# Two blocks of a projection moved ahead of the norm that feeds them, with scale and shift applied to the banks

## The chip, the cores and the metric

The kernel runs on one core of one Trainium2 chip. The metric is device microseconds (us) of one execution; the time of a kernel is the median over runs. Below, PE is TensorE, DVE is VectorE, ACT is ScalarE, POOL is GpSimd, and SP is SyncE, whose queue issues nearly all transfers. PEld is TensorE's weight load, which the profile lists beside PE.

## The reference, cut to what matters

Two transformer blocks run one after the other on 512 tokens of width 1024. The end of the first block and the start of the second are what the change touches:

```python
# end of the first block
x = x + square(relu(hm @ w_up)) @ w_down
x = rms_norm(x, norm_final)
# start of the second block
ada = silu(c) @ w_ada + b_ada
shift, scale, gate = split(ada, 3)
h = _rms(x, g_pre) * (1.0 + scale) + shift
proj = h @ w_in
q, k, v, z_a, u_b, v_b, z_b, g_logits = split(proj, SPLIT_IDX, axis=-1)
q = _rope(q, positions); k = _rope(k, positions)
```

So h is, token by token, x times a factor for the column (norm_final, g_pre and 1 + scale), times a factor for the token (the two norms together), plus a shift for the column. The projection has 38 blocks of 128 columns; block 4 is k and block 5 is v.

## The kernel before

Activations are held feature-major: a tile is 128 features by 512 tokens, and X has eight such tiles. A product of 1024 features into one block of 128 columns is 24 matmuls into one bank, because each operand is split into a high and a low part (whi and wlo for weights, made by L167 on ACT and L168 on DVE) and three of the four products are kept (L193, L194, L195 in mm_fm). Weights come in halves of a block, 128x512 values: wload takes a raw buffer (five of them), issues its transfer on SP (L185) and splits it into whi (four buffers) and wlo (three).

The last quarter of the MLP (qt = 3) runs over eight column blocks j. For each, after the 24 matmuls, DVE scales the bank (L908), adds it to X (L912) and squares it with a weight (L914, tile wsq); ACT squares X (L715), and POOL adds up both kinds of squares (L716 for the norm of the MLP's result, L918 for the weighted sum, facc). Then come, in the text: sums over the features by one-column matmuls with a vector of ones (L161, first facc, then the last square, flast), an inverse square root of nine small DVE steps after two setting-up ones (L149 to L154), its broadcast over the partitions by matmuls into a bank (L203, rrb), and eight times three operations that make h2: hf (L931, DVE), its high part (L932, ACT), its low part (L933, DVE). Next 32 transposes of X (L939), whose banks ACT copies (L941) for eight transfers to memory (L942), and then the projection: block 4 (k, through rope), block 5 (v), blocks 0 to 3 (q) and the others.

A scheduler in the compiler orders each engine's instructions ahead of time: it takes the earliest in the text whose inputs it expects to be ready. The order on each engine is then fixed; an instruction that isn't ready holds up all behind it on that engine. Big tiles come from a pool of seven regions, banks for products from a pool of three (mm), for small sums from a pool of two (sc), for transposes from a pool of three (ch).

Of the kernel before, what the change touches and what calls it, by code (L numbers as in the profile page):

```python
# [10 lines left out]
F32 = mybir.dt.float32  # L11
# [35 lines left out]
def fused_kernel(ctx, tc, a, out):  # L47
# [19 lines left out]
    def regionr(name):  # L67
        return reg.tile([128, 4, 2, T], F32R, tag="R", bufs=7, name=nm(name))

    def tmp(tag, shape=(128, T), dt=F32, bufs=1):  # L70
        return tp.tile(list(shape), dt, tag=tag, bufs=bufs, name=nm(tag))

    def tt(name, shape=(128, T), dt=F32):
        return tp.tile(list(shape), dt, tag="t", bufs=10, name=nm(name))
# [4 lines left out]
    def mmbank():  # L79
        return ps.tile([128, T], F32, tag="mm", bufs=3, name=nm("mm"))  # L80

    def scbank():
        return ps.tile([128, T], F32, tag="sc", bufs=2, name=nm("sc"))
# [55 lines left out]
    def vcol(name, i=0, n=1):  # L139
        o = VOFF[name] + i  # L140
        return vc[:, o:o + n]
# [3 lines left out]
    def rsqrt(src, n, scale, eps, tag=None):  # L145
        v = tmp("rq_v", (128, n), bufs=2)
        y = tmp(tag or "rq_y", (128, n), bufs=1 if tag else 3)
        t = tmp("rq_t", (128, n), bufs=2)
        V.tensor_scalar(v, src, scale, eps, op0=ALU.mult, op1=ALU.add)  # L149
        V.tensor_scalar(y.bitcast(I32), v.bitcast(I32), -0.5, RSQRT_SEED, op0=ALU.mult, op1=ALU.add)  # L150
        for _ in range(3):
            V.tensor_tensor(t, y, y, op=ALU.mult)
            V.scalar_tensor_tensor(t, t, -0.5, v, op0=ALU.mult, op1=ALU.mult)
            V.scalar_tensor_tensor(y, t, 1.5, y, op0=ALU.add, op1=ALU.mult)  # L154
        return y

    def sums(*accs):
        p = scbank()
        for i, acc in enumerate(accs):
            for tb in range(TB):  # L160
                PE.matmul(p[:, tb:tb + 1], lhsT=acc[:, tb * 128:(tb + 1) * 128], rhs=ones,  # L161
                          start=i == 0 and tb == 0, stop=i == len(accs) - 1 and tb == TB - 1)
        return p[:, 0:TB]

    def split(src, hi, lo, scale=None, eng=V):
        if scale is None:
            S.copy(hi, src)  # L167
            eng.tensor_tensor(lo, src, hi.bitcast(F32), op=ALU.subtract)  # L168
        else:
            S.activation(hi, src, AF.Copy, scale=scale)  # L170
            V.scalar_tensor_tensor(lo, src, scale, hi.bitcast(F32), op0=ALU.mult, op1=ALU.subtract)

    def wsplit(raw, shape):
        hi = wp.tile(shape, F32R, tag="whi", bufs=4, name=nm("whi"))
        lo = wp.tile(shape, F32R, tag="wlo", bufs=3, name=nm("wlo"))
        split(raw, hi, lo)
        return hi, lo

    def wload(tiles, k0, nk):
        ncol = tiles.shape[2]  # L180
        step = T // ncol
        parts = []
        for k in range(k0, k0 + nk, step):
            raw = wp.tile([128, step, ncol], F32, tag="wraw", bufs=5, name=nm("wraw"))
            nc.sync.dma_start(raw, tiles[:, k:k + step, :])  # L185
            hi, lo = wsplit(raw, [128, step, ncol])
            parts += [(hi[:, i, :], lo[:, i, :]) for i in range(step)]
        return parts
# [8 lines left out]
    def pairs(regs, n):  # L197
        return [(regs[i // 4][:, i % 4, 0, :], regs[i // 4][:, i % 4, 1, :]) for i in range(n)]

    def bcast(r):  # L200
        p = scbank()
        for tb in range(TB):
            PE.matmul(p[:, tb * 128:(tb + 1) * 128], lhsT=r[:, tb:tb + 1].to_broadcast([128, 128]), rhs=ident,  # L203
                      start=True, stop=True)
        return p
# [662 lines left out]
    def rope_tables():  # L868
# [14 lines left out]
        V.tensor_scalar(ropeC, ropeC, -2.0, 1.0, op0=ALU.mult, op1=ALU.add)  # L883
        V.tensor_scalar(ropeS, ropeS, rsign, None, op0=ALU.mult)

    for qt in range(4):
        ffx = pairs([regionr("ff0"), regionr("ff1")], DB)
        for j in range(DB):
            p = mmbank()
            mm_fm(p, wload(a["w_up"][qt * DB + j], 0, DB), x2g)  # L890
            u = tt("u")
            S.activation(u, p, AF.Relu)
            sq_ins = V.tensor_tensor(u, u, u, op=ALU.mult)
            split(u, ffx[j][0], ffx[j][1])
            if qt == 0 and j == 0:
                r2 = rsqrt(sums(n2.acc), TB, 1.0 / D, 1e-6, "r2")
                V.tensor_tensor(r2, r2, r2, op=ALU.mult)
                S.copy(r2b, bcast(r2))
                rope_tables()
            if qt < 3:  # L900
                ada_step(qt * DB + j, sq_ins.ins)
            elif j == 0:
                late_constants()
        for j in range(DB):
            p = mmbank()
            mm_fm(p, wload(a["w_down"][j], qt * DB, DB), ffx)
            d = tt("d")
            V.tensor_tensor(d, p, r2b, op=ALU.mult)  # L908
            if qt < 3:
                G.tensor_tensor(X[:, j], X[:, j], d, op=ALU.add)  # L910
            else:
                V.tensor_tensor(X[:, j], X[:, j], d, op=ALU.add)  # L912
                sq = tt("wsq")
                V.scalar_tensor_tensor(sq, X[:, j], wf[:, j:j + 1], X[:, j], op0=ALU.mult, op1=ALU.mult)  # L914
                if j == 0:
                    facc = sq
                elif j < DB - 1:
                    G.tensor_tensor(facc, facc, sq, op=ALU.add)  # L918
                else:
                    flast = sq  # L920
                nf1.add(X[:, j])


    rrb = bcast(rsqrt(sums(facc, flast), TB, 1.0 / D, 1e-12))
    acol = cst.tile([128, DB], F32, name="acol")
    V.scalar_tensor_tensor(acol, adac[:, 8:16], 1.0, vcol("g_pre", 0, DB), op0=ALU.add, op1=ALU.mult)
    V.tensor_tensor(acol, acol, vcol("norm_final", 0, DB), op=ALU.mult)
    h2 = pairs([regionr("h2a"), regionr("h2b")], DB)
    for j in range(DB):
        hf = tt("hf")  # L930
# [14 lines left out]
    def proj2(blk):  # L945
        p = mmbank()
        mm_fm(p, wload(a["w_in_2"][blk], 0, DB), h2)
        return p

    def rope(p):  # L950
        f = tt("rf")
        S.copy(f, p)
        sw = tt("rsw")
        for p0 in (0, 32, 64, 96):
            nc.sync.dma_start(sw[p0:p0 + 32], f[p0 ^ 32:(p0 ^ 32) + 32])
        G.tensor_tensor(sw, sw, ropeS, op=ALU.mult)
        V.tensor_tensor(f, f, ropeC, op=ALU.mult)
        V.tensor_tensor(f, f, sw, op=ALU.add)
        return f
# [1 line left out]
    kvr = regionr("kvr")  # L961
    khi, klo = kvr[:, 0], kvr[:, 1]
    G.memset(klo.bitcast(F32), 0.0)
    f = rope(proj2(4))
    for kv in range(2):
        rows = slice(64 * kv, 64 * kv + 64)
        S.copy(khi[rows, kv], f[rows])
        S.copy(khi[64 - 64 * kv:128 - 64 * kv, kv], f[rows])
        V.tensor_tensor(klo[rows, kv], f[rows], khi[rows, kv].bitcast(F32), op=ALU.subtract)
    vf = tt("vf")  # L970
    S.copy(vf, proj2(5))
    pv = scbank()
    for tb in range(TB):
        PE.transpose(pv[:, tb * 128:(tb + 1) * 128], vf[:, tb * 128:(tb + 1) * 128], ident)
# [282 lines left out]
```

## Time and profile before

| | us |
|---|---|
| median of 3 runs | 1328.11 |
| lowest and highest | 1325.77, 1330.02 |
| profiled execution, its own time | 1321.5 |
| its span, first to last instruction | 1319.5 |
| PE busy | 1290.2 (98%) |
| DVE busy | 829.1 (63%) |
| ACT busy | 530.4 (40%) |
| POOL busy | 166.3 (13%) |
| mean granted clock of PE | 0.995 |

The span is shorter than the execution's own time by 2.0 us, which lie around it. PE's busy time counts the tail of each matmul, so a matmul shown with 0.39 us may be followed 0.23 us later by the next; how many of them start in a stretch tells more than the busy share. All positions below are us from the start of the span.

### The profile page before, as it was taken

Reading aid. Unit: us, or ns where it says so; the run is one execution under the profiler, and the core shown is the slowest. Engines: PE = TensorE matmul, PEld = TensorE weight load, DVE = VectorE, ACT = ScalarE, POOL = GpSimd, SP = SyncE. Lnnn points to the kernel's source line nnn. Section 1 sums busy time; section 2 is a strip of 40 time slices with the busy share of each in tenths; the row PEclk is TensorE's granted clock in tenths of the full one; section 3 lists DMA queues with packets and bytes.
Section 4 is the critical chain, followed back from the end, with each engine's and each line's share of the span. In section 5 each row is a group of like instructions: output and inputs, shape, how many; then the busy total and the mean of one; then the engine's idle time right before and its main releaser. Section 6 shows DMA issues by size and latency. Waiting matters only on the chain.

```text
span 1319.5 us, 18273 instructions
## 1 busy us (share of the span) xinstructions
PE 1290.2 (98%) x6594; PEld 1061.5 (80%) x6594; DVE 829.1 (63%) x1657; ACT 530.4 (40%) x956; POOL 166.3 (13%) x178
## 2 busy tenths in 40 slices
PE   8989999999999999999999999999999999999997
PEld 6778888878889888888888888888878777788886
DVE  6867585857477665656845636544677666663356
ACT  6534332322344443544523323324345465333342
POOL 1222101020110020002021020120232000100003
PEclk9989999999999999999999999999999999999999
DMA  6111432323324522143544535323334223233331
GB/s 233 56 56 59 115 102 67 98 59 115 95 66 137 195 98 83 56 161 122 190 128 129 191 97 165 110 92 96 96 120 143 74 70 130 88 96 97 97 118 64
DMA packets 85498, 143.95 MB, mean 109 GB/s; under 512 B 21504, under 2 KB 21632, under 8 KB 85408
## 3 DMA queue, kind: packets, MB, share of 16 engines
q1 hardware_dynamic: 85408, 142.78, 34.7%
q8 instruction: 52, 0.85, 0.3%
q14 instruction: 38, 0.31, 0.1%
HBM read 136.19 MB, written 5.24 MB: 107 GB/s over the span
## 4 chain that ended last, share of the span: by engine, by line
PE 93%; DVE 5%; issue 1%; POOL 0%; DMA 0%; ACT 0%; SPq 0%; DVEq 0%; ACTq 0%; POOLq 0%
PE mm L193 25%; PE mm L194 25%; PE mm L195 25%; PE mm L686 1%; PE mm L687 1%; PE mm L685 1%; PE sc L445 1%; DVE wlo L168 1%; PE ch L1046 1%; PE ch L517 1%; PE ch L1011 1%; PE ch L550 1%; PE ch L521 1%; PE ch L526 1%; PE ch L502 1%
## 5 line engine op out<-in xcount | busy, mean ns | idle before, releaser
L167 ACT CAST whi<-wraw 128x512 fp32r<-128x512 f32 x398 | 246.5, 622 | 518.7 <-PE mm L194 452.8
L168 DVE TENSOR_TENSOR wlo<-wraw,whi 128x512 fp32r<-128x512 f32 x398 | 291.4, 734 | 206.7 <-PE mm L195 105.4
L193 PE MATMUL mm<-h,whi 128*128 128x512 f32 x296 | 118.3, 400 | 0.0
L194 PE MATMUL mm<-h,whi 128*128 128x512 f32 x296 | 117.1, 396 | 0.0
L195 PE MATMUL mm<-h,wlo 128*128 128x512 f32 x296 | 116.6, 394 | 0.0
L193 PE MATMUL mm<-x2g,whi 128*128 128x512 f32 x256 | 100.2, 391 | 0.0
L195 PE MATMUL mm<-x2g,wlo 128*128 128x512 f32 x256 | 99.7, 390 | 0.0
L194 PE MATMUL mm<-x2g,whi 128*128 128x512 f32 x256 | 99.6, 389 | 0.0
L193 PE MATMUL mm<-ff,whi 128*128 128x512 f32 x256 | 99.6, 389 | 0.0
L194 PE MATMUL mm<-ff,whi 128*128 128x512 f32 x256 | 99.6, 389 | 0.0
L195 PE MATMUL mm<-ff,wlo 128*128 128x512 f32 x256 | 99.6, 389 | 0.0
L910 POOL TENSOR_TENSOR X<-X,d 128x512 f32<-128x512 f32 x24 | 39.3, 1636 | 220.9 <-DVE d L908 220.9
L193 PEld LDWEIGHTS mm<-h,whi 128*128 128x128 f32 x296 | 55.9, 189 | 13.6 <-DVE k L287 1.1
L195 PEld LDWEIGHTS mm<-h,wlo 128*128 128x128 f32 x296 | 55.9, 189 | 11.8 <-issue 0.2
L194 PEld LDWEIGHTS mm<-h,whi 128*128 128x128 f32 x296 | 55.9, 189 | 11.2 <-issue 0.2
L716 POOL TENSOR_TENSOR gt<-gt,nsq 128x512 f32<-128x512 f32 x21 | 27.7, 1321 | 274.9 <-ACT nsq L715 267.4
L194 PE MATMUL mm<-h2a,whi 128*128 128x512 f32 x152 | 59.8, 393 | 0.5 <-DVE h2a L933 0.5
L193 PE MATMUL mm<-h2a,whi 128*128 128x512 f32 x152 | 59.4, 393 | 0.3 <-ACT h2a L932 0.3
L195 PE MATMUL mm<-h2a,wlo 128*128 128x512 f32 x152 | 59.7, 393 | 0.0
L193 PE MATMUL mm<-h2b,whi 128*128 128x512 f32 x152 | 59.6, 392 | 0.0
L195 PE MATMUL mm<-h2b,wlo 128*128 128x512 f32 x152 | 59.5, 392 | 0.0
L194 PE MATMUL mm<-h2b,whi 128*128 128x512 f32 x152 | 59.3, 391 | 0.0
(488 smaller groups left out, 2777.7 us busy)
## 6 DMA issues: line engine op xcount, KB each, us to landing
wraw<-in_w_in SPq DMA_DIRECT2D x162, 256.0 KB, 2.7
wraw<-in_w_up SPq DMA_DIRECT2D x64, 256.0 KB, 2.6
wraw<-in_w_down SPq DMA_DIRECT2D x64, 256.0 KB, 2.7
adaraw<-in_w_ada SPq DMA_DIRECT2D x24, 512.0 KB, 3.6
wraw<-in_w_proj_b SPq DMA_DIRECT2D x16, 256.0 KB, 2.6
wraw<-in_w_k SPq DMA_DIRECT2D x16, 256.0 KB, 2.7
wraw<-in_w_proj_a SPq DMA_DIRECT2D x16, 256.0 KB, 2.8
wraw<-in_w_v SPq DMA_DIRECT2D x16, 256.0 KB, 2.7
```

The lines of the kernel that those rows point to most:

```text
L167: S.copy(hi, src)
L168: eng.tensor_tensor(lo, src, hi.bitcast(F32), op=ALU.subtract)
L193: PE.matmul(acc, lhsT=wh, rhs=xh, start=start and k == 0, stop=False)
L194: PE.matmul(acc, lhsT=wh, rhs=xl, start=False, stop=False)
L195: PE.matmul(acc, lhsT=wl, rhs=xh, start=False, stop=stop and k == n - 1)
L445: PE.matmul(pq[hd % 2][:, j * 128:(j + 1) * 128], lhsT=KB[p0:p0 + 64, j, n * 128:(n + 1) * 128], rhs=AR[p0:p0 + 64, j, n].rearrange("p q c ...
L502: PE.matmul(pg[ub:ub + 64, hd * 64:(hd + 1) * 64], lhsT=gr[:, hd, 0:64], rhs=VU[:, tb, c, hd, :], start=hd == 0, stop=n == 0 and hd == 7)
L517: PE.matmul(pu[ub:ub + 32, hs], lhsT=ZT[ub:ub + 32, c, hd, :], rhs=gsb[ub:ub + 32, hs], start=True, stop=True)
L521: PE.matmul(pg[ub + 32:ub + 64, hd * 64:(hd + 1) * 64], lhsT=gr[ub:ub + 32, hd, 32:64], rhs=VU[ub:ub + 32, tb, c, hd, :], start=False, sto ...
L526: PE.matmul(pu[ub + 32:ub + 64, hs], lhsT=ZT[ub + 32:ub + 64, c, hd, :], rhs=gsb[ub + 32:ub + 64, hs], start=True, stop=True)
L716: G.tensor_tensor(self.acc, self.acc, sq, op=ALU.add)
L910: G.tensor_tensor(X[:, j], X[:, j], d, op=ALU.add)
```

## The change

Two blocks of the second projection, 4 and 5, no longer wait for h2. During the last quarter of the MLP, each finished tile of X is multiplied by its column factor acol and split into a high and a low part (xa, two regions); acol is computed before that loop instead of after it. Blocks 4 and 5 are products of w_in_2 with xa. What that leaves out is applied afterwards: each bank is multiplied by the token's factor rrb on DVE, and the shift's product with the block's weights is added as a bias by ACT. That product is made on PE: 8 matmuls of a block's raw weights (128x128) with one column of the shift, into a bank from which DVE copies one column. rrb is now copied from its bank into SBUF by ACT. The text computes block 4 ahead of the broadcast, block 5 behind it, and h2 behind both. The other 36 blocks use h2 as before.

```diff
-    def wload(tiles, k0, nk):
+    def wload(tiles, k0, nk, use=None):
...
             nc.sync.dma_start(raw, tiles[:, k:k + step, :])
+            if use is not None:
+                use(raw, k)
             hi, lo = wsplit(raw, [128, step, ncol])
...
+    acol = cst.tile([128, DB], F32, name="acol")
+    xa = []
     for qt in range(4):
+        if qt == 3:
+            V.scalar_tensor_tensor(acol, adac[:, 8:16], 1.0, vcol("g_pre", 0, DB), op0=ALU.add, op1=ALU.mult)
+            V.tensor_tensor(acol, acol, vcol("norm_final", 0, DB), op=ALU.mult)
...
                 nf1.add(X[:, j])
-
-
-    rrb = bcast(rsqrt(sums(facc, flast), TB, 1.0 / D, 1e-12))
-    acol = cst.tile([128, DB], F32, name="acol")
-    V.scalar_tensor_tensor(acol, adac[:, 8:16], 1.0, vcol("g_pre", 0, DB), op0=ALU.add, op1=ALU.mult)
-    V.tensor_tensor(acol, acol, vcol("norm_final", 0, DB), op=ALU.mult)
+                if j == 0:
+                    xa = pairs([regionr("xa0"), regionr("xa1")], DB)
+                split(X[:, j], xa[j][0], xa[j][1], scale=acol[:, j:j + 1])
+
+
+    shifts = tmp("shifts", (128, 2))
+
+    def unscaled(i, blk):
+        pc = scbank()
+
+        def use(raw, k0):
+            for k in range(k0, k0 + 4):
+                PE.matmul(pc[:, 0:1], lhsT=raw[:, k - k0], rhs=adac[:, k:k + 1], start=k == 0, stop=k == DB - 1)
+
+        w = wload(a["w_in_2"][blk], 0, DB, use)
+        V.tensor_copy(shifts[:, i:i + 1], pc[:, 0:1])
+        p = mmbank()
+        mm_fm(p, w, xa)
+        return p
+
+    def rescaled(i, p):
+        f = tt("rf")
+        V.tensor_tensor(f, p, rrb, op=ALU.mult)
+        S.activation(f, f, AF.Identity, bias=shifts[:, i:i + 1])
+        return f
+
+    rr = rsqrt(sums(facc, flast), TB, 1.0 / D, 1e-12)
+    pk4 = unscaled(0, 4)
+    rrb = tt("rrb")
+    S.copy(rrb, bcast(rr))
+    pv5 = unscaled(1, 5)
     h2 = pairs([regionr("h2a"), regionr("h2b")], DB)
...
-    def rope(p):
-        f = tt("rf")
-        S.copy(f, p)
+    def rope(p, f=None):
+        if f is None:
+            f = tt("rf")
+            S.copy(f, p)
...
-    f = rope(proj2(4))
+    f = rope(None, rescaled(0, pk4))
...
-    vf = tt("vf")
-    S.copy(vf, proj2(5))
+    vf = rescaled(1, pv5)
```

## Rows read from the trace of the kernel before

**Rows 1.** The page: the chain that ended last, share of the span by engine.

```profile
PE 93%; DVE 5%; issue 1%; POOL 0%; DMA 0%; ACT 0%; SPq 0%; DVEq 0%; ACTq 0%; POOLq 0%
```

**Rows 2.** Timeline of PE: start, length, engine, line, operation, count, idle before.

```profile
966.96 0.39 PE L195 MATMUL mm<-ff,wlo 128*128 128x512 f32 x1
...
969.00 0.39 PE L195 MATMUL mm<-ff,wlo 128*128 128x512 f32 x1
969.91 1.05 PE L161 MATMUL sc<-ones,wsq 128*128 128x1 f32 x8 [0.52 <-POOL wsq L918]
970.82 1.51 PE L939 MATMUL ch<-ident,X 128*128 128x128 f32 x12
972.23 1.05 PE L161 MATMUL sc<-ones,wsq 128*128 128x1 f32 x8
973.15 1.71 PE L939 MATMUL ch<-ident,X 128*128 128x128 f32 x12
976.27 1.16 PE L203 MATMUL sc<-ident,rq_y 128*128 128x128 f32 x8 [1.41 <-DVE rq_y L154]
977.49 1.28 PE L939 MATMUL ch<-ident,X 128*128 128x128 f32 x8
979.10 0.73 PE L193 MATMUL mm<-h2a,whi 128*128 128x512 f32 x2 [0.34 <-ACT h2a L932]
...
985.02 0.39 PE L193 MATMUL mm<-h2b,whi 128*128 128x512 f32 x1
...
992.99 0.95 PE L161 MATMUL sc<-ones,gt 128*128 128x1 f32 x8
993.80 0.48 PE L194 MATMUL mm<-h2a,whi 128*128 128x512 f32 x1
```

**Rows 3.** L193, L194, L195 in a stretch: its length, PE busy (matmuls), clock, DMA share, GB/s.

```profile
969.20:985.00 15.80, 2.92 (x8) 1.00 0.43 156
...
969.20:985.00 15.80, 2.85 (x7) 1.00 0.43 156
...
969.20:985.00 15.80, 2.75 (x8) 1.00 0.43 156
```

**Rows 4.** Timeline of DVE: one block of the MLP's last quarter.

```profile
959.76 0.69 DVE L912 TENSOR_TENSOR X<-X,d 128x512 f32<-128x512 f32 x1
960.48 0.75 DVE L914 SCALAR_TENSOR_TENSOR wsq<-X,wf 128x512 f32<-128x512 f32 x1
961.33 1.84 DVE L168 TENSOR_TENSOR wlo<-wraw,whi 128x512 fp32r<-128x512 f32 x1
964.06 0.69 DVE L908 TENSOR_TENSOR d<-mm,gt 128x512 f32<-128x512 f32 x1 [0.89 <-PE mm L195]
964.67 0.68 DVE L168 TENSOR_TENSOR wlo<-wraw,whi 128x512 fp32r<-128x512 f32 x1
```

**Rows 5.** Timeline of POOL, same block.

```profile
961.32 1.30 POOL L716 TENSOR_TENSOR gt<-gt,nsq 128x512 f32<-128x512 f32 x1 [2.45 <-DVE wsq L914]
962.58 1.74 POOL L918 TENSOR_TENSOR wsq<-wsq,wsq 128x512 f32<-128x512 f32 x1
```

**Rows 6.** Timeline of DVE after that loop, to the end of h2.

```profile
971.43 0.75 DVE L914 SCALAR_TENSOR_TENSOR wsq<-X,wf 128x512 f32<-128x512 f32 x1
973.33 0.16 DVE L149 TENSOR_SCALAR rq_v<-sc 128x4 f32<-128x4 f32 x1 [1.15 <-PE sc L161]
...
977.54 2.07 DVE L931 SCALAR_TENSOR_TENSOR hf<-X,acol,sc 128x512 f32<-128x512 f32 x3 [1.33 <-PE sc L203]
...
987.39 1.50 DVE L933 SCALAR_TENSOR_TENSOR h2b<-hf,adac,h2b 128x512 fp32r<-128x512 f32 x2
```

**Rows 7.** Timeline of SP's queue.

```profile
972.62 9.57 SPq L942 DMA_DIRECT2D xf_d<-xo  x8
987.51 3.55 SPq L185 DMA_DIRECT2D wraw<-in_w_in  x3
```

**Rows 8.** L932 on ACT: count, duration in ns (least/median/most), first and last start.

```profile
L932 ACT ACTIVATE h2a<-hf,adac x4: 721/723/726, 978.3 to 982.3; 128x512 fp32r<-128x512 f32 x4
```

## The prediction

> **What bounds the kernel now.** I read the page's chain first: 93% of the span is PE, nearly nothing is transfers [rows 1]. So only what PE does, or waits for, counts, and I went to PE's timeline at the border between the MLP and the second projection [rows 2]. There the reader should look at starts, since a length holds the tail of a matmul. Inside the MLP ten matmuls start between 966.96 and 969.00, nine steps in 2.04 us: 0.227 us a matmul, 24 x 0.227 = 5.44 us a block, at a clock of 1.00 [rows 2, 3]. The last MLP matmul has its slot until 969.23. From 985.02 on PE is again in that step.
>
> In the 15.79 us between, 22 block matmuls start (23 are counted, one of them the tail of the 969.00 one) [rows 3]: 22 x 0.227 = 4.99 us. The sums are 16 entries, two for each of 8 matmuls, at (973.15 - 972.23) / 8 = 0.115 us: 1.84. The transposes are 12 + 12 + 8 at (972.23 - 970.82) / 12 = 0.118: 3.76. The broadcast is 8 entries, at the price of the sums 0.92 [rows 2]. Together 11.5, so PE stands idle for 15.8 - 11.5 = 4.3 us: at the end of the MLP for the POOL sum, while DVE does the inverse square root, and for the first pieces of h2. That is all the change can win here; 4.3 us is 0.33% of 1321.5.
>
> **What the change removes.** With xa of seven column blocks ready when the loop ends, PE has 21 matmuls of block 4 at hand (4.8 us) before it needs xa of the last one, then block 5. Its last tile of X is squared until 972.18 [rows 6]; ACT's part of the split (0.72, [rows 8]) and DVE's (0.75, as L914 [rows 4]) end near 974, and PE comes to it at 969.23 + 1.84 + 4.8 or later: covered. I keep the first wait, 969.23 to 969.91 for POOL [rows 2], because the sum of facc stands ahead of block 4 in the text: 0.7. Removed: 4.3 - 0.7 = 3.6 us; bounds 2.2 (see the order rival) and 4.3.
>
> **What it adds on PE.** Sixteen matmuls of 128x128 fp32 weights with one column. Their nearest row is the sum L161, the same shape: two entries each, 32 entries. The rows give 0.115 us an entry, or (993.80 - 992.99) / 8 = 0.101 where the next block's matmul follows [rows 2]. So 3.2 to 3.7 us; I take 3.6, since both rows within the gap give 0.114 and 0.115. PE is what sets the end here, so with the idle time gone nothing hides them. This is the heart of the forecast: one gap is filled, and three quarters of its length or more is paid again for the shift.
>
> The Trainium skill speaks of this price in "TensorE: Matmul & The Clock Gate", section Back-to-back issue gap: for 1 to 64 columns about 60 cycles, an issue floor of 25 ns. By that figure alone 32 entries would take 0.8 us, an estimate, and the sum would be 2.8 us lower; the rows of L161 do not bear it out. It is the third rival below.
>
> **What it adds in the MLP's loop.** Per block j one ACT operation of 0.72 us, which has room (ACT is busy for 40% of the span, and never the chain's engine [rows 1]), and one DVE operation of 0.75 us with two inputs in SBUF. DVE's idle time before L908 is 0.89 us a block, so at first sight it fits by 0.14 [rows 4]. But POOL stands in the way: L168 at 961.33 takes 1.84 us instead of 0.68, ending 0.55 us after POOL's L716 ends, and POOL's L918 in turn takes 1.74 [rows 4, 5]. Added up as if these excluded each other, a block has L912 0.69, L914 0.75 and two L168 of 0.68 on DVE, 2.80 us, and on POOL 1.30 and, from the end of L168 at 963.17 to 964.32, 1.15: 5.25 of 5.44 us. With 0.75 more it is 6.0, so 0.56 us too much in each of the six blocks that have both POOL operations, a lag of 3.4 us at the end. L168 is what PE could wait for: it ends at 963.17 and its first user is the fifth L195 of the next block, at 966.96 [rows 2, 4], 3.8 us later. So the lag stays inside the margin, if narrowly, and I put 0 for the loop; bounds 0 and 3.2 (rival below).
>
> The Trainium skill's page "GPSIMD Engine Reference", section Specifications, says that POOL's SBUF interfaces are shared with VectorE, with contention for DVE instructions that have two SBUF inputs; it would put all four of DVE's operations above, and the new one, against POOL. That speaks against this change, and the 1.84 us agree with it.
>
> **Behind the loop.** Half of the lag, 1.7 us, on DVE moves the last square to 973.9. From there as before: 1.15 to the first inverse-root step, 4.2 from that to the first hf [rows 6], 0.7 for ACT's new copy of rrb: 980.0. The sixteen DVE operations of h2 took 977.54 to 988.89 with one L168 among them, 10.7 without; with three splits of 0.68 h2 is whole at 992.7. PE meanwhile: 969.23 + 0.7 + 1.8 (sums) + 10.9 (blocks 4 and 5) + 3.6 + 0.9 = 987.1, and 990.9 after the transposes. Its first h2 block wants the last tile of h2 4.8 us later, at 995.7, or at 991.9 if the transposes are put behind: a wait of 0 or 0.8. I take 0.5. Then come two DVE passes of 0.69 over the banks; ACT's bias pass takes the place of a copy. The rope of block 4 is needed only by the attention, seven blocks on. The banks of 4 and 5 are let go near 994 instead of being copied at once; three mm banks let PE go on to the end of the first h2 block, 992 to 996, so this may cost a few tenths and no more.
>
> **Queues.** The raw tiles of the two blocks are held until PE has used them. Before, SP's next weight issue after the border came only at 987.51, behind the eight writes of X [rows 7], and PE didn't wait for weights. Now the first of the held buffers is free when PE has done half a block of one-column matmuls, near 971, sixteen us ahead of the first h2 block at 987: 0. If the transposes come late, the writes do too, and weights behind them on SP wait; three halves ahead are 3 x 2.72 = 8.2 us of cover.
>
> **Sum.** -3.6 + 3.6 + 0 + 0.5 = +0.5 us on the profiled 1321.5: 1322.0. The median of the runs lies 0.5% above the profiled execution (1328.11 to 1321.5), so the forecast on its scale is 1328.6.
>
> **The rivals.**
> *DVE and POOL saturate (slower).* If the new operation waits for a whole POOL operation of 1.3 each time, a block needs 0.75 + 1.3 - 0.89 = 1.16 us more than it has, 7.0 over six blocks, 3.2 beyond the 3.8 of margin: PE stalls on wlo, and h2 comes up to 2.9 us late behind it. +3.2 to +6.1, middle 4.7: 1326.2, or 1332.8 on the median's scale. It decides from 0.63 us of lag a block. For it: 5.25 of 5.44 already. Against: POOL's sums aren't urgent and can take the delay. Chance 0.22.
> *The order undoes it.* If PE's fixed order puts the second sum ahead of block 4, PE waits until 972.23 as now, with only the first sum to do: 2.1 us idle remain. Removed 2.2, added 3.6, and the 0.5: +1.9, 1323.4 or 1330.0. The scheduler already drew transposes ahead of that sum [rows 2], which speaks against it. Chance 0.12.
> *The one-column matmuls cost next to nothing (faster),* their weight loads going under the 512-column stream: -3.6 + 0 + 0.5 = -3.1, 1318.4 or 1325.0. For it: 0.101 instead of 0.115 where a block follows. Chance 0.08.
> *The balance above:* 0.58; its own range is -1.1 (all 4.3 removed, 3.2 paid) to +3.
>
> **Numbers.** A measurement here can't tell less than about 0.3%, 4 us, from no change. Faster takes a third of the third rival and little of the rest: 0.06. Slower takes most of the first rival, 0.17, and 0.05 of the others: 0.22. The same: 0.72. The range from 1324.5 to 1334.0 holds the balance and the order rival, most of the third and the first up to its upper part.
>
> **What the new profile should show.** L193 on xa starting within a microsecond or two of the last MLP matmul; no wait of PE for L154, L932 or L933; 32 new entries at 0.10 to 0.12 us; L168 or the new split at 1.3 us or more where POOL runs; wlo in time. I am wrong if PE waits for L168 inside the loop, if the first h2 block waits for L933, or if the new entries take 0.03 us.

## The result, and the profile after

The change made the kernel slower by half a per cent: 1333.99 us (median of 20 runs, 1327.65 to 1336.96) against 1327.38 for the kernel before (20 runs, 1321.11 to 1330.42). The ratio is 1.0051, interval 1.0036 to 1.0065, so 6.6 us. The time lies within the range that was given, at its upper end; the forecast itself, no measurable change, was wrong.

The profiled execution of after took 1329.73 us with a span of 1328.0, 8.5 more than before's. Line numbers of after: 195 to 197 are the three products of a block's matmul (193 to 195 before), 915, 919 and 921 DVE's three operations of a column block (908, 912, 914), 718 and 925 POOL's sums (716, 918), 171 the low part of xa, 941 the one-column matmuls with the shift, 944 the copy of their column, 205 the broadcast.

The chain that ended last, shares of the span, answers to [rows 1]:

```profile
PE 90%; DVE 7%; issue 1%; ACT 1%; POOL 0%; DMA 0%; SPq 0%; DVEq 0%; ACTq 0%; POOLq 0%
```

PE still sets the end, but DVE's share went up from 5 to 7%. The first block's whole MLP takes the same time in both (352.6 and 352.7 us from its first to its last matmul), and so does everything from the first score matmul of the second block's attention on (283.6 in both). Two stretches make up the 8.5 us. One is in the state scan of the first block, 4.1 us, where both kernels have the same instructions in the same order and only the granted clock differs:

```profile
200.00:300.00 100.00, 98.26 (x690) 80.85 (x689) 60.48 (x151) 26.63 (x45) 15.24 (x22) 0.96 0.27 71
```

The columns are the window, its length, busy time and count of PE, PE's weight loads, DVE, ACT and POOL, then PE's granted clock, the DMA share and GB/s. The clock is 0.96; in before's window it is 1.00, though the change touches nothing there. Both kernels' executions spread over some 10 us, and I count this with that spread and not with the change. The other 4.4 us lie between the last MLP matmul and the first score matmul: 66.9 us before (969.0 to 1035.9), 71.3 after (973.1 to 1044.4). The first score matmul, before and after:

```profile
1035.86 0.33 PE L1011 MATMUL ch<-kvr,qr 128*128 128x128 f32 x2
1044.43 0.33 PE L1043 MATMUL ch<-kvr,qr 128*128 128x128 f32 x2
```

Everything below is about this stretch.

PE's timeline there answers to [rows 2]; a bracket holds the recorded idle time and its releaser:

```profile
973.06 0.39 PE L197 MATMUL mm<-ff,wlo 128*128 128x512 f32 x1
974.71 1.05 PE L161 MATMUL sc<-ones,wsq 128*128 128x1 f32 x8 [1.26 <-POOL wsq L925]
975.63 1.93 PE L941 MATMUL sc<-adac,wraw 128*128 128x1 f32 x16
977.41 0.69 PE L195 MATMUL mm<-xa,whi 128*128 128x512 f32 x1
977.90 0.63 PE L196 MATMUL mm<-xa,whi 128*128 128x512 f32 x1
978.32 0.63 PE L197 MATMUL mm<-xa,wlo 128*128 128x512 f32 x1
...
981.14 0.40 PE L195 MATMUL mm<-xa,whi 128*128 128x512 f32 x1
...
986.72 1.16 PE L205 MATMUL sc<-ident,rq_y 128*128 128x128 f32 x8
987.72 1.84 PE L941 MATMUL sc<-adac,wraw 128*128 128x1 f32 x16
989.42 0.48 PE L197 MATMUL mm<-xa,wlo 128*128 128x512 f32 x1
...
1018.95 0.39 PE L196 MATMUL mm<-h2b,whi 128*128 128x512 f32 x1
1020.27 0.50 PE L197 MATMUL mm<-h2b,wlo 128*128 128x512 f32 x1 [0.93 <-DVE wlo L168]
```

Four things are to be seen, each measured from start to start with 0.227 us for a block matmul's slot, as in the prediction.

- **The wait for POOL** behind the MLP is there, twice as long: the last slot ends at 973.29, the sum starts at 974.71, so 1.42 us instead of 0.68.
- **The one-column matmuls** take 977.41 - 975.63 = 1.78 and 989.42 - 987.72 = 1.70 us for 16 entries each: 3.48.
- **The block matmuls behind them step at half pace**: from 977.41 to 981.14 nine of them take 3.73 us instead of 9 x 0.227 = 2.04, a loss of 1.69. The steps of 0.42 and 0.43 us are near twice 0.227.
- **A new wait for wlo** at 1020.27: 1020.27 - 1018.95 - 0.227 = 1.09 us.

That the pace is the clock is seen in the windows, with the columns as above:

```profile
968.00:974.00 6.00, 5.45 (x25) 4.17 (x23) 5.94 (x8) 2.86 (x5) 3.97 (x3) 1.00 0.06 24
974.00:980.00 6.00, 5.29 (x30) 4.74 (x31) 2.37 (x5) 0.94 (x2) 0.83 (x2) 0.79 0.24 76
980.00:986.00 6.00, 6.00 (x30) 5.05 (x29) 3.03 (x12) 1.45 (x3) 2.00 (x2) 0.92 0.04 14
986.00:992.00 6.00, 6.00 (x39) 5.12 (x38) 3.03 (x8) 2.22 (x5) 0.00 (x0) 1.00 0.40 128
```

The granted clock is full until the MLP's end, means of 0.79 and 0.92 stand in the next two windows, which is part of the time at the lower of its two levels (1.2 instead of 2.4 GHz), and then it is full again. In before it is 1.00 from 969.2 to 985 [rows 3], and in every later window of the stretch.

The sum: idle slots of before in this stretch come to 0.68 (POOL) + 1.72 (inverse root) + 0.28 (behind the broadcast) + 0.67 and 0.78 (first pieces of h2) = 4.13. After has 1.42 + 3.48 + 1.69 + 1.09 = 7.68, and 0.57 in three small gaps (0.13 ahead of the broadcast, 0.20 and 0.24 around transposes). 7.68 + 0.57 - 4.13 = +4.1 of the 4.4.

Why POOL is late is in the loop's timeline of DVE, which answers to [rows 4], and of POOL, to [rows 5]:

```profile
964.35 0.68 DVE L919 TENSOR_TENSOR X<-X,d 128x512 f32<-128x512 f32 x1
965.07 0.75 DVE L921 SCALAR_TENSOR_TENSOR wsq<-X,wf 128x512 f32<-128x512 f32 x1
965.74 0.68 DVE L168 TENSOR_TENSOR wlo<-wraw,whi 128x512 fp32r<-128x512 f32 x1
966.41 1.72 DVE L171 SCALAR_TENSOR_TENSOR xa<-X,acol,xa 128x512 fp32r<-128x512 f32 x1
968.12 0.69 DVE L915 TENSOR_TENSOR d<-mm,gt 128x512 f32<-128x512 f32 x1
968.73 1.11 DVE L168 TENSOR_TENSOR wlo<-wraw,whi 128x512 fp32r<-128x512 f32 x1
969.76 0.68 DVE L919 TENSOR_TENSOR X<-X,d 128x512 f32<-128x512 f32 x1
```

```profile
965.90 1.68 POOL L718 TENSOR_TENSOR gt<-gt,nsq 128x512 f32<-128x512 f32 x1 [2.02 <-DVE wsq L921]
967.54 1.74 POOL L925 TENSOR_TENSOR wsq<-wsq,wsq 128x512 f32<-128x512 f32 x1
971.31 1.67 POOL L718 TENSOR_TENSOR gt<-gt,nsq 128x512 f32<-128x512 f32 x1 [2.03 <-DVE wsq L921]
972.93 1.73 POOL L925 TENSOR_TENSOR wsq<-wsq,wsq 128x512 f32<-128x512 f32 x1
```

The split of xa meets POOL as L168 did before: 1.72 us instead of the 0.75 of L921, a form with as many operands. It ends 0.55 us after L718, as L168 ended 0.55 after L716 in [rows 4, 5]. DVE has no idle time left before L915. Yet it keeps pace: from one L919 to the next it is 969.76 - 964.35 = 5.41 us, no more than PE's 5.44 for a block. The L168 that stands beside POOL's first addition takes 0.68 now instead of 1.84; the split behind it is what is lengthened. POOL pays too. Two additions stand one behind the other after each square; the pair of this block takes 3.38 us, that of [rows 5] 3.00. The last pair is what PE's sum waits for. Before's was:

```profile
966.82 1.79 POOL L716 TENSOR_TENSOR gt<-gt,nsq 128x512 f32<-128x512 f32 x1 [2.51 <-DVE wsq L914]
968.57 1.29 POOL L918 TENSOR_TENSOR wsq<-wsq,wsq 128x512 f32<-128x512 f32 x1
```

It started 2.41 us ahead of the end of the MLP's last slot and took 3.04. After's started 1.98 ahead of it and took 3.35, to 974.66; PE's sum starts at 974.71. So 0.43 us of the longer wait are DVE's later square, and 0.31 are POOL's longer pair. The Trainium skill's "GPSIMD Engine Reference", section Specifications, tells of this contention without a size; here it is about 1 us for one DVE operation and 0.4 for a pair of POOL's additions.

### The profile page after: what moved, and what is told of

It is laid out like the page before. It is cut to its first block, busy times and chain, and to the rows that moved or that the text cites. A ratio compares the mean times of both kernels' runs of the same rounds, so it can differ in the third digit from the quotient of the medians.

```text
span 1328.0 us, 18354 instructions
## 1 busy us (share of the span) xinstructions
PE 1299.0 (98%) x6626; PEld 1068.7 (80%) x6626; DVE 837.6 (63%) x1669; ACT 535.4 (40%) x965; POOL 168.6 (13%) x178
## 4 chain that ended last, share of the span: by engine, by line
PE 90%; DVE 7%; issue 1%; ACT 1%; POOL 0%; DMA 0%; SPq 0%; DVEq 0%; ACTq 0%; POOLq 0%
PE mm L195 24%; PE mm L197 24%; PE mm L196 24%; DVE wlo L168 2%; PE mm L688 1%; PE mm L687 1%; PE mm L689 1%; PE sc L447 1%; PE ch L1078 1%; PE ch L519 1%; PE ch L528 1%; DVE xa L171 1%; PE ch L552 1%; PE ch L1043 1%; PE ch L523 1%
## 5 line engine op out<-in xcount | busy, mean ns | idle before, releaser
L168 DVE TENSOR_TENSOR wlo<-wraw,whi 128x512 fp32r<-128x512 f32 x398 | 289.4, 730 | 206.9 <-PE mm L197 106.1
L195 PE MATMUL mm<-h,whi 128*128 128x512 f32 x296 | 118.7, 401 | 0.0
L195 PE MATMUL mm<-x2g,whi 128*128 128x512 f32 x256 | 100.2, 391 | 0.0
L195 PE MATMUL mm<-ff,whi 128*128 128x512 f32 x256 | 99.6, 389 | 0.0
L195 PEld LDWEIGHTS mm<-h,whi 128*128 128x128 f32 x296 | 56.2, 190 | 13.7 <-DVE k L289 1.1
L718 POOL TENSOR_TENSOR gt<-gt,nsq 128x512 f32<-128x512 f32 x21 | 29.2, 1393 | 276.4 <-ACT nsq L717 270.3
L197 PE MATMUL mm<-h2b,wlo 128*128 128x512 f32 x144 | 56.7, 394 | 1.0 <-DVE wlo L168 0.9
L197 PE MATMUL mm<-h2a,wlo 128*128 128x512 f32 x144 | 56.6, 393 | 0.0
L195 PE MATMUL mm<-h2a,whi 128*128 128x512 f32 x144 | 56.6, 393 | 0.0
L195 PE MATMUL mm<-h2b,whi 128*128 128x512 f32 x144 | 56.6, 393 | 0.0
L196 PE MATMUL mm<-h2a,whi 128*128 128x512 f32 x144 | 56.5, 393 | 0.0
L196 PE MATMUL mm<-h2b,whi 128*128 128x512 f32 x144 | 56.4, 392 | 0.0
```

The lines of the kernel that those rows point to most:

```text
L195: PE.matmul(acc, lhsT=wh, rhs=xh, start=start and k == 0, stop=False)
L196: PE.matmul(acc, lhsT=wh, rhs=xl, start=False, stop=False)
L197: PE.matmul(acc, lhsT=wl, rhs=xh, start=False, stop=stop and k == n - 1)
L718: G.tensor_tensor(self.acc, self.acc, sq, op=ALU.add)
```

## The experiments

The ratios below are to the kernel before on the same chips, with 95% intervals. "Stretch" is from the last MLP matmul to the first score matmul in the profile, 66.9 us before and 71.3 after, with both starts read to 0.1 us. The last column has the granted clock of the two windows of 6 us that begin with the last MLP matmul (the first profile of after was shown above in windows that begin 1 us later, 0.79 and 0.92). One caution for the ratios: a kernel whose stretch is before's to 0.1 us (the fourteenth row) measured 1.0016, so two ratios that differ by 0.002 aren't told apart, and the stretch is the finer measure.

| kernel | median, us | before there | ratio | stretch | clock behind the MLP |
|---|---|---|---|---|---|
| after, first profile | 1333.99 | 1327.38 | 1.0051 [1.0036, 1.0065] | 71.3 | .87, .85 |
| after again, twice | 1326.49, 1329.45 (one run each) | 1327.6 | | 71.4, 73.0 | .85, .87; .71, .73 |
| after without the shift | 1327.55 | 1327.8 | 1.0011 [0.9993, 1.0030] | 67.4 | .81, .90 |
| before + split | 1330.11 | 1327.8 | 1.0016 [0.9998, 1.0035] | 68.8 | .82, .61 |
| before + one-column matmuls | 1330.18 | 1327.8 | 1.0018 [1.0000, 1.0035] | 69.4 | 1.00 |
| after, copies late | 1334.37 | 1327.8 | 1.0038 [1.0019, 1.0057] | 72.3 | .85, .87 |
| after, POOL's sum first | 1329.17 | 1326.24 | 1.0017 [0.9995, 1.0038] | 70.1 | .83, .89 |
| no shift, POOL's sum first | 1325.44 | 1326.24 | 0.9987 [0.9968, 1.0006] | 64.4 | 1.00 |
| one block on xa, POOL's sum first | 1325.26 | 1326.24 | 0.9996 [0.9976, 1.0016] | 66.2 | 1.00 |
| before, constants in the gap | 1329.19 | 1326.24 | 1.0017 [0.9998, 1.0037] | 70.4 | 1.00 |
| interleaved, POOL's sum first | 1337.11 | 1327.58 | 1.0073 [1.0046, 1.0100] | other order | 1.00 |
| interleaved | 1341.59 | 1327.58 | 1.0109 [1.0080, 1.0138] | other order | .84, .88 |
| before + split, POOL's sum first | 1322.88 | 1327.58 | 0.9983 [0.9963, 1.0003] | 66.9 | 1.00 |
| before, POOL's sum first | 1328.31 | 1327.58 | 1.0016 [0.9999, 1.0033] | 66.8 | 1.00 |
| interleaved, scores pinned | 1338.45 | 1327.6 | 1.0071 [1.0043, 1.0099] | 75.0 | 1.00 |
| columns behind each block, POOL's sum first | 1328.17 | 1327.18 | 1.0003 [0.9983, 1.0024] | 67.2 | 1.00 |

### First: which part costs

**After without the shift.** The one-column matmuls and their copies go; ACT adds another column, which costs the same. k and v lack the shift.

```diff
...
-                PE.matmul(pc[:, 0:1], lhsT=raw[:, k - k0], rhs=adac[:, k:k + 1], start=k == 0, stop=k == DB - 1)
-
-        w = wload(a["w_in_2"][blk], 0, DB, use)
-        V.tensor_copy(shifts[:, i:i + 1], pc[:, 0:1])
+        w = wload(a["w_in_2"][blk], 0, DB)
...
-        S.activation(f, f, AF.Identity, bias=shifts[:, i:i + 1])
+        S.activation(f, f, AF.Identity, bias=adac[:, i:i + 1])
```

> The change without the shift's product: the 16 one-column matmuls and the two copies of their column are left out, and the bias of blocks 4 and 5 is another column of the same size, so that k and v lack their shift. Theory 1 (the one-column matmuls are what costs: 32 entries of 0.11 us, 3.5 us, and behind them nine block matmuls at half the granted clock, 1.6 us): the changed kernel's excess of 6.6 us falls by 5 or more, to between -1 and +1.5 us against the kernel before, and the clock of the stretch behind the MLP stays 1.00. Theory 2 (the split's second operation in the MLP's loop is what costs, by DVE and POOL shutting each other out): the excess stays at +3 us or more. Theory 3 (the copies of the shift's column hold DVE's queue) expects a fall too, with DVE's two waits of 3.3 and 2.9 us gone; the next run but two tells it from theory 1.

The stretch is 67.4, 3.9 less than after's, near the 3.5 of the entries. Yet with 4.1 of idle time to win and nothing paid for the shift it should have been well under before's 66.9. PE waits 1.42 for POOL here too, and the clock fell:

```profile
975.30:981.30 6.00, 4.74 (x21) 3.69 (x20) 3.46 (x5) 1.87 (x3) 3.74 (x3) 0.81 0.28 85
```

**Before + split.** Only xa is made, and acol ahead of it; nobody uses xa.

```diff
...
                 nf1.add(X[:, j])
+                if j == 0:
+                    xa = pairs([regionr("xa0"), regionr("xa1")], DB)
+                split(X[:, j], xa[j][0], xa[j][1], scale=acol[:, j:j + 1])
```

> The kernel before, with only the scaled split of X into xa added to the MLP's last quarter (16 operations, nothing reads xa). Theory 1: within 1 us of the kernel before, since wlo has 3.8 us of margin. Theory 2: slower by 3 us or more. Either way the last MLP matmul is followed by a longer wait for POOL's sum than the 0.7 us of before, if the late sum (1.4 us in the changed kernel) comes from the split.

1.9 us of stretch. The wait for POOL is after's, with the sums and transposes behind it instead of one-column matmuls, and the clock falls there as well:

```profile
978.11 1.05 PE L161 MATMUL sc<-ones,wsq 128*128 128x1 f32 x8 [1.24 <-POOL wsq L923]
```

```profile
976.50:982.50 6.00, 4.76 (x33) 4.39 (x32) 3.78 (x8) 3.31 (x6) 3.73 (x3) 0.82 0.37 124
```

**Before + one-column matmuls**, ahead of blocks 4 and 5, which stay on h2.

```diff
+        if blk in (4, 5):
...
+            w = wload(a["w_in_2"][blk], 0, DB, use)
+            V.tensor_copy(shifts[:, blk - 4:blk - 3], pc[:, 0:1])
```

> The kernel before, with only the 16 one-column matmuls of blocks 4 and 5 and the two copies added (nothing reads the result). Theory 1: slower by about 3.5 us, less what falls into the 4.1 us in which PE stands idle there (the first eight may: then 1.8 to 3.5). If the half clock comes from such matmuls too, it shows in the window behind the MLP. Theory 2: within 1 us.

2.5 us of stretch, at full clock, for 32 entries: each sixteen take 1.71 us (984.43 to 986.14, 995.63 to 997.34), about what the rows of L161 said. Together that is 3.42, less what of before's idle time they cover, and nothing like the 0.8 of the third rival.

**After, copies late.** DVE's queue showed a suspect: the copy of the first block's column waits 3.34 us for PE, and the next one 2.93, with h2 behind it.

```profile
977.59 0.16 DVE L944 COPY shifts<-sc 128x1 f32<-128x1 f32 x1 [3.34 <-PE sc L941]
989.60 0.16 DVE L944 COPY shifts<-sc 128x1 f32<-128x1 f32 x1 [2.93 <-PE sc L941]
```

So both columns went to one bank, copied by one operation behind the last piece of h2.

```diff
...
-        V.tensor_copy(shifts[:, i:i + 1], pc[:, 0:1])
...
+        if i == 0:
+            with tc.issue_after(h2_ins.ins):
+                V.tensor_copy(shifts, pc[:, 0:2])
```

> The changed kernel, with the shift's two columns in one bank and copied in one operation put behind h2 on DVE, so that no copy stands ahead of the last tile of X or of h2 in DVE's queue. Theory 3 (the copies' wait costs): faster than the changed kernel by 2 us or more, h2 begins 6 us earlier. Theory 1: within 1 us of the changed kernel, because PE has blocks 4 and 5 to do meanwhile; the 32 entries and the half clock stay.

72.3 and 1.0038: no gain. The copies' waits of six us are gone, but h2 starts no earlier: 16.8 us behind the MLP's last slot, against 16.4 in after, because it waits for rrb now. This theory fell.

### Second: the wait, the clock and the columns

**After, POOL's sum first.** The addition of facc goes ahead of the other one on POOL; every other engine keeps its order.

```diff
-                    G.tensor_tensor(facc, facc, sq, op=ALU.add)
+                    fadd = G.tensor_tensor(facc, facc, sq, op=ALU.add)
...
-                nf1.add(X[:, j])
+                if j:
+                    with tc.issue_after(fadd.ins):
+                        nf1.add(X[:, j])
+                else:
+                    nf1.add(X[:, j])
```

> The changed kernel with one thing else: on POOL each addition to facc is put ahead of the addition for the MLP norm instead of behind it. Theory A (the split makes facc late on POOL, PE stands still for 1.4 us at the end of the MLP instead of 0.7, and the granted clock is halved behind that): PE's wait falls under 0.7 us, the clock of the 12 us behind the MLP is 1.00, and the stretch from the last MLP matmul to the first score matmul falls from 71.3 to 69 us or less; against the kernel before the excess falls from 6.6 to 3 to 4 us, the price of the columns. Theory B (the clock is halved because of the one-column matmuls): the wait falls, the clock stays halved for some 3 us and the stretch falls by 0.7 to 1 us only.

The wait is gone and the stretch is 1.2 us shorter, 70.1, but the clock fell all the same:

```profile
975.54 0.40 PE L197 MATMUL mm<-ff,wlo 128*128 128x512 f32 x1
975.78 0.95 PE L161 MATMUL sc<-ones,wsq 128*128 128x1 f32 x8
976.59 1.93 PE L945 MATMUL sc<-adac,wraw 128*128 128x1 f32 x16
```

```profile
975.50:981.50 6.00, 6.00 (x36) 5.28 (x36) 3.02 (x6) 1.86 (x3) 2.05 (x2) 0.83 0.32 90
981.50:987.50 6.00, 6.00 (x29) 4.92 (x27) 3.51 (x13) 1.24 (x2) 1.46 (x2) 0.89 0.00 0
```

Eight block matmuls from 979.39 to 982.73 took 3.34 us instead of 1.82, a loss of 1.5. By the profile PE is busy all through these windows. What stands in for the wait is 24 one-column entries in a row, 2.6 us from 975.78. So my theory that the wait alone brings the lower clock fell.

**The same without the shift** (k and v lack it) takes the columns away too.

> The change without the shift's product (16 one-column matmuls, two copies and the true bias left out) and with facc first on POOL. Theory A: clock 1.00 behind the MLP, stretch of 67.4 falling to 65 us or less, faster than the kernel before by 1 to 3 us. Theory B expects the clock back at 1.00 as well, but no more than that the run without columns had it, that is halved; then the stretch stays at 66.5 or more.

The clock stays at 1.00 and the stretch is 64.4: 2.5 under before's, in spite of a later wait of 1.13 us for split weights. This is the gain that the moved blocks have without the shift's price.

**One block on xa** (block 5 back on h2), the columns strewn between block 4's matmuls, the copy late, POOL's sum first.

```diff
...
-        mm_fm(p, w, xa)
+        for k in range(DB):
+            mm_fm(p, w[k:k + 1], xa[k:k + 1], start=k == 0, stop=k == DB - 1)
+            PE.matmul(pc[:, i:i + 1], lhsT=raws[k // 4][:, k % 4], rhs=adac[:, k:k + 1], start=k == 0, stop=k == DB - 1)
...
-    vf = rescaled(1, pv5)
+    vf = tt("vf")
+    S.copy(vf, proj2(5))
```

> The best form of the change that the runs so far point to: only block 4 runs on xa, each one-column matmul stands behind the three matmuls of its column block, the shift is copied late, facc comes first on POOL. Eight one-column matmuls cost 1.8 us, and 5.4 us of block 4 fill most of the 4.1 us of idle time: the stretch comes to 64.5 to 66 us against 66.9, 1 to 2.4 us faster than the kernel before. If the idle time is only moved behind block 4 (h2 not ready), it is 67 or more and the kernel is not faster.

66.2 at full clock, 0.7 under before's; 0.9996, no change that can be measured.

**Before, constants in the gap.** A rival use of the idle time: other work (late_constants) moved from the start of the MLP's last quarter to behind the inverse root.

```diff
-            elif j == 0:
-                late_constants()
...
-    rrb = bcast(rsqrt(sums(facc, flast), TB, 1.0 / D, 1e-12))
+    rr = rsqrt(sums(facc, flast), TB, 1.0 / D, 1e-12)
+    late_constants()
+    rrb = bcast(rr)
```

> The kernel before with late_constants (16 broadcast entries, two 512-column fp32 matmuls and their splits) moved from the start of the MLP's last quarter to the end of it, where PE stands idle for 4.1 us; nothing of the change is in it. If idle time there can be filled with work that needs no price: about 2.5 us of PE work goes into the gap, and the kernel is 1.5 to 2.5 us faster than the kernel before. If DVE is what is waited for there (its extra operations of the constants stand ahead of h2), it is the same or slower by 1 to 3 us.

The MLP is 2.6 us shorter, the stretch 3.5 longer, net +0.9: what left the MLP came back in full and more, and the waits for the inverse root (1.14) and for pieces of h2 are still there.

### Third: what is left without wait and columns

**Interleaved**, after with both blocks' columns strewn between their matmuls as above, with POOL's sum first and without.

> The changed kernel, both blocks, with each one-column matmul behind the three matmuls of its column block, the shift copied late, and facc first on POOL. If the clock was halved because 24 one-column entries stood in a row behind the MLP (theory B, which the run with facc first alone spoke for): clock 1.00 behind the MLP, the stretch from the last MLP matmul to the first score matmul at 68 to 69 us, against 70.1 with the columns in a row; the excess over the kernel before falls to 1.5 to 2.5 us, which is the columns' 3.5 us less the idle time removed, plus waits for weights. If the clock has another cause it stays halved, and the stretch at 70.

> The same without facc first on POOL: PE waits 1.4 us for POOL's sum again. If that wait alone halves the clock, as the run without columns suggests, the clock behind the MLP is halved for about 3 us here although no columns stand in a row, and the stretch is 2.2 to 3 us longer than in the run with facc first. If the wait is harmless by itself, only 1.4 us longer at clock 1.00.

The clock went as hoped behind the MLP (1.00 and, with the wait of 1.44, .84). But both kernels are slower than after, for another reason: the order that the compiler fixes put the score matmuls behind 120 projection matmuls instead of 240, where PE waited 2.69 and 3.57 us for the rotated q. They tell nothing of the change's own time.

**Before + split, POOL's sum first**, and **before, POOL's sum first**, ask what the split costs when no wait follows from it.

> The kernel before with the split of X alone, and facc first on POOL. If the split costs only through POOL's late sum and the clock behind it: clock 1.00, a stretch of 66 to 67 us as in the kernel before, time within 1 us of it. If DVE's fuller queue costs by itself (theory 2): the stretch stays near 68.8 us and the time 2 us or more above.

> The kernel before with facc first on POOL and nothing else: PE's wait of 0.7 us at the end of the MLP goes, but PE then waits as long for the last square, so the stretch stays within 0.5 us of 66.9 and the time does not change by what can be measured.

66.9 and 66.8: the split of xa costs DVE a microsecond each time and PE nothing, once PE doesn't wait for the sum. The kernel with the split differs from the one above (68.8) in the order on POOL alone, and its clock is full:

```profile
970.00:976.00 6.00, 5.25 (x42) 4.71 (x41) 4.41 (x9) 3.31 (x6) 3.92 (x4) 1.00 0.33 114
```

**Interleaved, scores pinned** behind the tenth projection block, to undo that shift of order.

```diff
...
-                        PE.matmul(pk[kv][:, i * 256:i * 256 + W], lhsT=qr[:, j, kv, qs], rhs=kx[:, kv, ks],
+                        with tc.issue_after(z_last.ins):
+                            PE.matmul(pk[kv][:, i * 256:i * 256 + W], lhsT=qr[:, j, kv, qs], rhs=kx[:, kv, ks],
...
```

> The run with both blocks, columns between the block matmuls and facc first on POOL, with the score matmuls held behind the tenth projection block, where all other kernels but the two interleaved ones have them (there they came after 120 projection matmuls instead of 240, and PE waited for the rotated q). If the columns are all that is left to pay: clock 1.00 behind the MLP, the stretch from the last MLP matmul to the first score matmul at 68 to 69 us, an excess over the kernel before of 1.5 to 2.5 us. If running two blocks early has a price of its own (h2, the rope and the weights later), the stretch is 70 us or more.

A miss: PE now waits for split weights, which stand on ACT behind the work for the rope:

```profile
1015.73 0.80 PE L197 MATMUL mm<-h2a,whi 128*128 128x512 f32 x1 [4.50 <-ACT whi L167]
```

**After again**, two single executions, asks whether the lower clock is there each time.

> The changed kernel once more, for a second profile. In the first one the stretch behind the MLP explains 4.4 of the 6.6 us. If the rest lies in that stretch, in executions in which the clock stays halved for longer, a second execution shows a stretch longer than 71.3 us; if it lies elsewhere, the stretch is 71 to 71.6 us again and the clock of the earlier stages differs.

> The changed kernel a third time; the same expectation as for the second profile.

It is, and its cost varies. In the second of them it fell within the columns, so 16 entries took 977.34 - 973.92 = 3.42 us instead of 1.78, and eight block matmuls were slow behind them, 977.34 to 980.73, 1.57 over: 3.2 us together.

```profile
972.89 1.18 PE L161 MATMUL sc<-ones,wsq 128*128 128x1 f32 x8 [1.26 <-POOL wsq L925]
973.92 3.55 PE L941 MATMUL sc<-adac,wraw 128*128 128x1 f32 x16
977.34 0.77 PE L195 MATMUL mm<-xa,whi 128*128 128x512 f32 x1
...
980.73 0.40 PE L197 MATMUL mm<-xa,wlo 128*128 128x512 f32 x1
```

**Columns behind each block, POOL's sum first.** The whole change, with each block's eight one-column matmuls in one row behind its 24 instead of ahead; the later orders are nearly after's.

```diff
...
+        raws = []
+        w = wload(a["w_in_2"][blk], 0, DB, lambda raw, k0: raws.append(raw))
         p = mmbank()
         mm_fm(p, w, xa)
+        for k in range(DB):
+            PE.matmul(pc[:, 0:1], lhsT=raws[k // 4][:, k % 4], rhs=adac[:, k:k + 1], start=k == 0, stop=k == DB - 1)
+        V.tensor_copy(shifts[:, i:i + 1], pc[:, 0:1])
         return p
```

> The changed kernel with both blocks, facc first on POOL, and each block's eight one-column matmuls behind its 24 block matmuls instead of ahead of them; queue orders after that are those of the changed kernel but for a few exchanged neighbours, and the score matmuls stay behind 240 projection matmuls. If the columns' place (in a row straight behind the MLP) halved the clock: clock 1.00 behind the MLP, the stretch from the last MLP matmul to the first score matmul at 68 to 69 us, and the excess over the kernel before 1.5 to 2.5 us. If any row of them does: clock halved behind the first row, the stretch at 70 us.

67.2, ratio 1.0003. All 32 entries are still paid (the first 16 in 1.70 us), there is no wait behind the MLP, and the clock is full:

```profile
975.99 0.40 PE L197 MATMUL mm<-ff,wlo 128*128 128x512 f32 x1
976.23 0.95 PE L161 MATMUL sc<-ones,wsq 128*128 128x1 f32 x8
977.04 0.48 PE L195 MATMUL mm<-xa,whi 128*128 128x512 f32 x1
...
983.51 1.84 PE L948 MATMUL sc<-adac,wraw 128*128 128x1 f32 x16
985.21 0.49 PE L195 MATMUL mm<-xa,whi 128*128 128x512 f32 x1
```

```profile
976.00:982.00 6.00, 6.00 (x36) 5.25 (x35) 4.68 (x9) 2.49 (x4) 3.48 (x3) 1.00 0.00 0
982.00:988.00 6.00, 6.00 (x40) 5.41 (x39) 2.22 (x12) 0.45 (x1) 0.00 (x0) 1.00 0.40 110
```

It is 0.3 us longer in this stretch than before; the forecast's sum was +0.5. The interval of its ratio ends at 1.0024, below the 1.0036 at which after's begins, so the runs too show it faster than after. No version that computes everything clearly beats the kernel before: the lowest ratio, 0.9983 of before with an unused split, reaches to 1.0003.

## Why the prediction was wrong

**The balance was right.** Idle time swapped for the shift's product at equal price, 3.6 against 3.6: the waits for the inverse root and for h2 (3.45 us of before's slots) are gone but for small gaps, and the 32 entries took 3.48. The last kernel shows the swap by itself, 67.2 against 66.9. The third rival, entries that cost next to nothing, is out; the order rival too, since twelve matmuls of block 4 run ahead of the second sum and hide it.

**The step that failed** is the treatment of the lag: "I keep the first wait, 969.23 to 969.91 for POOL [rows 2] ...: 0.7", together with "So the lag stays inside the margin, if narrowly, and I put 0 for the loop". That POOL's and DVE's operations would lengthen each other was foreseen; but the lag was followed only to wlo, PE's user within the loop, and of POOL's sums the prediction said that they "aren't urgent and can take the delay". The last of them is urgent: PE's first instruction behind the MLP waits for it, 1.42 us instead of 0.68. Moving that sum ahead on POOL takes 1.2 us off the stretch. The size of the lag was wrong as well. It was to grow by 0.56 us in each of six blocks, to 3.4, because POOL's and DVE's times were added up as if they excluded each other; in fact DVE is full but keeps PE's pace (5.41 us a block), and at the end POOL's pair starts only 0.43 us later. So PE's loop was not delayed.

**What had no term at all** is the granted clock behind the MLP: 1.69 us of half pace in the first profile, 3.2 in the third. It hangs on what PE does behind the last MLP matmul, as the experiments show together. It fell in all seven profiles with a wait of 1.4 us there, with the row of the shift's entries behind it (after, three times, and the late copies) or without that row (no shift, split only, and interleaved). In three of these kernels POOL's order alone was then changed (no shift, split only, interleaved): the wait went, and the clock was 1.00. It also fell in the one profile with 24 one-column entries in a row and no wait (POOL's sum first). In the ten profiles with neither it was 1.00 behind the MLP. For after itself, removing either alone left the lower clock in place. The wait is shown well; the row rests on one profile, and a fall by chance isn't excluded there, since in the state scan the same instructions had 1.00 in one execution and 0.96 in another. With wait and row both out of the way, the stretch lost a further 2.9 us from POOL's sum first (70.1) to the columns behind the blocks (67.2), 1.5 of them half pace.

**The tail** was put at 0.5 and measured 1.09, in another place: not the first h2 block, which shows no wait but small gaps, but a wlo 25 us later, where DVE is busy for 10.75 of 12 us (1010 to 1022) in after. In the last kernel a wait for wlo of 0.75 is left, nearer to the estimate.

**The sum, term by term.** To the forecast's +0.5 the wait for POOL adds 0.74, the half pace 1.69, the tail 0.59 and the small gaps 0.57, which makes +4.1. None of the three signs by which the prediction was to know that it was wrong appeared: no wait for L168 inside the loop, none of the first h2 block for h2, and no entries of 0.03 us. It had looked for failure in the wrong places.

**The slower rival** had DVE and POOL saturate, and named "h2 late" and a wlo within the loop as the places where it would be paid. DVE is full there, but it keeps pace, and neither was paid. Its middle, 1332.8, is near the measured median by luck, through other terms.

**What stays open.** The stretch accounts for 4.4 us in the first profile and 6.1 in the one with the longest half clock, the measured difference is 6.6, with an interval from about 4.8 to 8.6. The clocks of the runs allow an estimate of the rest. Each run has its span and its mean granted clock, to 0.001, which is 1.3 us. If the missing share of the clock counts as lost time, after's 20 runs lost 16.9 us of a mean span of 1331.5, and 35 runs of before, taken with the first experiments, 12.8 of 1324.9. By this some 4 us of the difference are clock, anywhere in the span, and some 2.5 work and waits, about what the first profile's stretch has without its half pace (4.4 - 1.7). Where the clock's part beyond this stretch lies isn't known. How often an execution has the long form isn't known from three profiles, nor why before's wait of 1.72 us behind transposes kept the full clock while 1.4 us behind the MLP did not.

## What to carry to other kernels

When work is moved into an idle gap of the engine that sets the end, price first what the move adds on that same engine; here it was the whole gain. Then follow a lag on helper engines to every waiter, not only to the one inside the loop: the one that paid here was a small sum behind it. And try narrow matmuls behind dense ones where the order is free: here 16 one-column entries ahead of a block, behind a row of sums, were followed by 1.5 us of half pace, and the same entries behind the block by none. That is one profile of each.

## What the hardware showed that was not expected

- The granted clock fell to its lower level behind the MLP in all seven profiles with a wait of 1.4 us at that place, and in the one with 24 one-column entries in a row there, though PE had run dense until then; it cost 1.6 to 3.2 us in after. It is not a rule for all places: in after, the broadcast's eight 128-column entries with 16 one-column entries behind them (986.72 to 989.42, between block matmuls) kept 1.00, and so did the wait of 1.09 at 1020.27, and before's waits and transposes. Longer waits further on, 2.69 and 3.57 us for the rotated q and 4.65 for split weights, brought it down as well: the windows of 6 us around them have 0.74, 0.54 and 0.62.
- In after both additions of a POOL pair took 1.67 to 1.75 us, in all but the first pair; in before one of the two took 1.74 or 1.79 and the other 1.29 or 1.30. So both engines lose when they meet. With facc first on POOL, DVE has 0.27 or 0.34 us of idle time before L915 in each of the last four blocks, where after has at most 0.03: here the order of two additions on one engine decides how full the other is.
